# The sums of weights in a Strassen step: four instructions or three, into a tile of their own or in place

## The chip, the cores and the metric

The kernel runs on one core of a Trainium2 chip. The metric is the device time of one execution in microseconds (us), and the median over the runs is compared. A core has five engines with instruction streams of their own: TensorE (PE in the profile; PEld is its loading of the stationary operand), VectorE (DVE), ScalarE (ACT), GpSimd (POOL) and SyncE (SP). Here SP only issues loads from HBM, one after another in one queue.

## The reference, cut to what matters

Two decoder layers over a residual stream h of 256 rows and 2048 columns, all float32. Each layer adds a mixer (attention and mLSTM in layer 0, forgetting attention in layer 1), and then an FFN with 5632 hidden columns. The FFN is where the change lies:

```python
def swiglu(xn, w_gate, w_up, w_down):
    return (jax.nn.silu(xn @ w_gate) * (xn @ w_up)) @ w_down
...
h = h + swiglu(rms_norm(h, norm_ffn[layer]), w_gate[layer], w_up[layer], w_down[layer])
```

So per layer there are three large products: 256 x 2048 by 2048 x 5632 twice, and 256 x 5632 by 5632 x 2048.

## The kernel before, in words

**Products in three parts.** A float32 number is written as a high half, rounded to TensorE's fast fp32r format, and a low half, the rest. A product of two matrices is then three matmuls: high by high, high by low, low by high (`three`, lines 531 to 534; the same in `gemm`, lines 222 to 224). The weights are split as they come in. SP loads a raw tile of 128 partitions and 2 x 512 elements, which is two blocks of 128 rows of the weight side by side (`load_raw`, line 134). ScalarE makes the high half (line 187, or 356 in `split_plain`), VectorE the low half by a subtraction (line 188 or 357). Both halves go into a slot, a pair of tiles named hi and lo. In the FFNs there are eight such slots, and a slot is free again once TensorE has read it.

**Pairs of column blocks.** `pair_group` (lines 539 to 635) makes two blocks of 512 output columns together: one of w_gate and one of w_up, or two of w_down. It goes through the inner dimension in pairs of 128-row blocks; the list `order` says which pair comes at which position, and whether it is a plain one (0) or a Strassen one (1). At a plain position each weight tile is split and multiplied as it is: eight block products of three matmuls. At a Strassen position the 2 x 2 blocks of inputs (two row blocks by two inner blocks) and the 2 x 2 blocks of weights are combined so that seven block products do. The sums of the inputs are made in `sums_of` (lines 272 to 275), once, and used for all columns. The sums of the weights are made anew at each position by VectorE. With a first weight tile `ra` (two inner blocks of the first column block) and a second one `rb`, lines 607 to 610 make ta to td. In the FFNs ta and tb go to a tile of their own, `t4`, and tc and td over `ra`. Then `t4` and `ra` are split like weights. The old `rb` is only read, last by line 609.

At the end `combine` (lines 553 to 570) puts the seven products together from four banks of PSUM: line 555 copies one with ScalarE, and lines 557 to 559 add the others with VectorE.

In the two mixers the same function runs with `halves` given: there the sums are made in place in `ra` and `rb` already, by four instructions, and split into a spare part of the tiles mh and ml. `x95` in the profile is the FFNs' number of Strassen positions, and `x14` and `x6` are the mixers'.

**What sets the order.** The code is written out as a straight line of instructions, and a planner orders each engine's instructions when the program is built, by a priority that follows the text and by a simulated time line; it places the waits too. Waits for a buffer follow from the pools: raw tiles at Strassen positions of the FFN come from the pool's tag "raw" with RAWS buffers (4), raw tiles at plain positions from the pool `wr` with 4 buffers, `t4` has one buffer. The FFN runs in three parts of 3, 4 and 4 column pairs (PARTS, 0, 3, 7, 11; the first of a part is g0): the part's gate and up columns first, then its share of w_down. Of the list ORDER positions 1, 3 and 5 are Strassen ones, and the shorter DOWN[6] of the first part has 1 and 3.

Of the kernel before, what the change touches and what calls it, by code (L numbers as in the profile page):

```python
# [7 lines left out]
F32 = mybir.dt.float32  # L8
# [4 lines left out]
ALU = mybir.AluOpType  # L13
# [4 lines left out]
P = 128  # L18
# [5 lines left out]
NB = 512  # L24
CK = 2
# [11 lines left out]
HEAVY = ((1, 1), (0, 0), (1, 3), (0, 2), (1, 5), (0, 4), (1, 7), (0, 6))  # L37
FOURTH = 7
DENSE = ()
DOWN = {  # L40
    6: ((0, 0), (1, 1), (0, 2), (1, 3), (0, 4), (0, 5)),
    8: ((0, 0), (1, 1), (0, 2), (1, 3), (0, 4), (1, 5), (0, 6), (0, 7)),
# [9 lines left out]
W_RAWS = 4  # L52
LATER = (6, 10, 3, 5)
LATER_DOWN = (5, 6)
RAWS = 4
P_JOIN = 4
COLD = 9
TURNED = (0,)
# [17 lines left out]
def trunk(  # L76
# [19 lines left out]
    nc = tc.nc  # L96
# [141 lines left out]
    sums = {}  # L238
# [24 lines left out]
    def sums_of(pool, sh, sl, copies, full=None, tags=("tmp", "tmp"), bufs=None, box=None, x4=None):  # L263
        if box is not None:
            full, s = box[:, 0:4, :].rearrange("p (i t) q -> p i t q", i=2), box[:, 4:8, :]
            copies(full.rearrange("p i t q -> p i (t q)"))
        elif full is None:
            full = pool.tile([P, 2, NT, P], F32, tag=tags[0], name="full", bufs=bufs)
            copies(full.rearrange("p i t q -> p i (t q)"))
        if box is None:  # L270
            s = pool.tile([P, 4, P], F32, tag=tags[1], name="s4", bufs=bufs)
        nc.vector.tensor_tensor(out=s[:, 0, :], in0=full[:, 0, 1, :], in1=full[:, 1, 1, :], op=ALU.add)
        nc.vector.tensor_tensor(out=s[:, 1, :], in0=s[:, 0, :], in1=full[:, 0, 0, :], op=ALU.subtract)
        nc.vector.tensor_tensor(out=s[:, 2, :], in0=full[:, 0, 0, :], in1=full[:, 0, 1, :], op=ALU.subtract)
# [264 lines left out]
    def pair_group(fp, par, lhs, sums, mats, order, todo=(), halves=None, inner=None, raws=None):  # L539
        plain = [[bank(par, "acc") for _ in range(NT)] for _ in range(2)]  # L540
        begun = set()

# [5 lines left out]
        todo = list(todo)  # L548
# [4 lines left out]
        def combine(prods):  # L553
            c = fp.tile([P, 4, NB], F32, tag="c", name="c", bufs=1)
            nc.scalar.copy(c[:, 0, :], prods[0])
            if halves is None:
                nc.vector.tensor_tensor(out=c[:, 1, :], in0=prods[3], in1=c[:, 0, :], op=ALU.add)
                nc.vector.tensor_tensor(out=c[:, 2, :], in0=prods[2], in1=c[:, 1, :], op=ALU.add)
                nc.vector.tensor_tensor(
                    out=c[:, 1:4:2, :],  # L560
                    in0=prods[1].rearrange("p (a n) -> p a n", a=1).broadcast_to([P, 2, NB]),
                    in1=c[:, 1:3, :],
                    op=ALU.add,
                )
                return c
            nc.vector.tensor_tensor(out=c[:, 2, :], in0=prods[3], in1=c[:, 0, :], op=ALU.add)
            nc.vector.tensor_tensor(out=c[:, 1, :], in0=prods[2], in1=c[:, 2, :], op=ALU.add)
            nc.vector.tensor_tensor(out=c[:, 3, :], in0=prods[1], in1=c[:, 1, :], op=ALU.add)
            nc.vector.tensor_tensor(out=c[:, 2, :], in0=prods[1], in1=c[:, 2, :], op=ALU.add)
            return c  # L570

        for pos, (kind, pair) in enumerate(order):
# [21 lines left out]
            if first:  # L594
                prods = [bank(1 - par, "prod") for _ in range(4)]
            ra, rb = (load_raw(w, k0, c0, NB, fp, W_RAWS if halves else RAWS, raws) for w, c0 in mats)
            hg, lg = split_chunk(ra, NB)
            run_due(todo, pos)
            t4 = ra if halves else fp.tile([P, 2, NB], F32, tag="t4", name="t4", bufs=1)
            ta, tb, tc_, td = (  # L600
                (ra[:, 0, :], rb[:, 0, :], rb[:, 1, :], ra[:, 1, :])
                if halves
                else (t4[:, 0, :], t4[:, 1, :], ra[:, 0, :], ra[:, 1, :])
            )
            hu, lu = slot()
            split_plain(hu[:, 1, :], lu[:, 1, :], rb[:, 1, :])
            nc.vector.tensor_tensor(out=ta, in0=rb[:, 0, :], in1=ra[:, 0, :], op=ALU.subtract)
            nc.vector.tensor_tensor(out=tb, in0=rb[:, 1, :], in1=rb[:, 0, :], op=ALU.subtract)
            nc.vector.tensor_tensor(out=tc_, in0=rb[:, 1, :], in1=ta, op=ALU.subtract)
            nc.vector.tensor_tensor(out=td, in0=ra[:, 1, :], in1=tc_, op=ALU.subtract)  # L610
            parts = []
            for src in (ra, rb) if halves else (t4, ra):
                if halves:
                    hs, ls = halves.pop(0)
                    halves.append((hs, ls))
                else:
                    hs, ls = slot()
                split_plain(hs, ls, src)
                parts.append((hs, ls))
# [17 lines left out]
    def ffn(layer, fp, sx, x4, sd, key, todo, idx_next=None, key_next=None, finish=None):  # L637
# [8 lines left out]
        for g0, g1 in zip(PARTS, PARTS[1:]):  # L646
# [3 lines left out]
            for g in range(g0, g1):  # L650
# [91 lines left out]
            for n0 in (0, 2):  # L742
                if end and idx_next is None and n0 == 2:
                    for n in (2, 3):
                        acc = new_acc()
                        gemm(acc, m_of, wd, n * NB, NB, 0, nk, nk, skew=3 if n == 3 else 1, halved=n == 3)
                        close(acc, n)
                    continue
                plain, c = pair_group(
                    fp, 1 - n0 // 2, m_of, sums_d, [(wd, n0 * NB), (wd, (n0 + 1) * NB)], order, todo  # L750
                )
# [625 lines left out]
```

## Time and profile before

| | us |
|---|---|
| median of three runs | 2077.59 |
| lowest and highest | 2077.39, 2079.51 |
| the profiled execution, its own time | 2077.56 |
| its span, from the first to the last instruction | 2075.9 |
| TensorE busy / VectorE busy / ScalarE busy | 2065.7 / 1819.0 / 1373.7 |
| granted TensorE clock | 0.999 |

How to read the profile: a group's row has the line of the kernel, the engine, the operation, out<-in by the program's names, the shapes and the count; behind the first bar busy time in us and the mean in ns of one; behind the second the engine's idle time just before them and what ended it. A row of the waits view has the waiting instruction, who released it, the total in us, how often, and the longest. A row of the time line has the start and the length in us. A row of the chain has the start, the length and what it was. "lo<-t,hi" is the low half of the tile t4, because buffer numbers are left out of names. Busy times are unions: two instructions that overlap for a moment count once. Layer 0's FFN lies between about 322 and 1010 us of the span, layer 1's begins at about 1380.

### The profile page before, as it was taken

The page shows a single profiled execution, that of the slowest core. Times are in us where ns is not written, and L with a number is a line of the kernel's source. Part 1 is how long each engine was busy: PE and PEld are TensorE (multiplying, and loading weights), DVE is VectorE, ACT ScalarE, POOL GpSimd, SP SyncE. Part 2 cuts the span into 40 slices and gives each one's busy share as a digit, 9 for nine tenths or more (in the row PEclk, how much of TensorE's full clock was granted, in tenths as well). Part 3 has the DMA queues.
Part 4 walks back from the last instruction along what each step waited for, and adds up shares of the span by engine and source line. Part 5 has one row for each costly group of instructions (what it writes and reads, how often), then busy time and mean ns, then how long its engine had stood idle before and what let it go on. Part 6 is the DMA issues. An engine that isn't in the chain of part 4 may idle for free.

```text
span 2075.9 us, 26965 instructions
## 1 busy us (share of the span) xinstructions
PE 2065.7 (100%) x9473; PEld 1715.1 (83%) x9473; DVE 1819.0 (88%) x2367; ACT 1373.7 (66%) x1744; POOL 44.6 (2%) x66
## 2 busy tenths in 40 slices
PE   9999999999999999999999999999999999999998
PEld 7878888888888888888888888888888888888886
DVE  6788769999999999999899688689999999999994
ACT  6777678664676656667676776687655666556763
POOL 1010000000000000000000001000000000000000
PEclk9999999999999999999999999999999999999999
DMA  8566577666677666766676776586756677667764
GB/s 292 169 216 192 188 244 238 206 219 196 210 223 224 193 208 217 222 204 183 206 213 209 231 201 183 155 268 217 233 187 218 209 217 224 202 195 225 206 196 141
DMA packets 309576, 434.88 MB, mean 209 GB/s; under 512 B 106412, under 2 KB 114624, under 8 KB 309312
## 3 DMA queue, kind: packets, MB, share of 16 engines
q1 hardware_dynamic: 307088, 426.27, 66.1%
q0 software_dynamic: 1632, 5.80, 0.8%
q8 instruction: 74, 1.21, 0.2%
q10 hardware_dynamic: 720, 1.09, 0.2%
q14 instruction: 62, 0.51, 0.1%
HBM read 408.68 MB, written 2.12 MB: 198 GB/s over the span
## 4 chain that ended last, share of the span: by engine, by line
PE 97%; DVE 1%; ACT 1%; issue 1%; DMA 0%; POOLq 0%; POOL 0%; ACTq 0%; DVEq 0%
PE acc L532 21%; PE acc L534 21%; PE acc L533 21%; PE acc L223 6%; PE acc L222 6%; PE acc L224 6%; PE prod L532 5%; PE prod L533 5%; PE prod L534 5%; PE p L386 1%; PE po L487 1%; ACT s L420 0%; PE po L488 0%; DVE lo L188 0%; DMA raw<-in_w_down_dram 0%
## 5 line engine op out<-in xcount | busy, mean ns | idle before, releaser
L188 DVE TENSOR_TENSOR lo<-raw,hi 128x1024 fp32r<-128x1024 f32 (+3 forms) x656 | 771.1, 1195 | 135.5 <-ACT hi L187 133.0
L187 ACT CAST hi<-raw 128x1024 fp32r<-128x1024 f32 (+3 forms) x656 | 661.7, 1027 | 341.2 <-PE acc L534 137.2
L533 PE MATMUL acc<-lo,xh 128*128 128x512 f32 x1320 | 514.0, 389 | 0.0
L534 PE MATMUL acc<-hi,xl 128*128 128x512 f32 x1320 | 511.4, 389 | 0.0
L532 PE MATMUL acc<-hi,xh 128*128 128x512 f32 x1320 | 506.2, 390 | 0.0
L534 PEld LDWEIGHTS acc<-hi,xl 128*128 128x128 f32 x1320 | 247.8, 188 | 51.6
L533 PEld LDWEIGHTS acc<-lo,xh 128*128 128x128 f32 x1320 | 247.8, 188 | 51.4 <-issue 0.2
L532 PEld LDWEIGHTS acc<-hi,xh 128*128 128x128 f32 x1320 | 247.7, 188 | 51.3 <-issue 0.2
L356 ACT CAST hi<-raw 128x512 fp32r<-128x512 f32 x204 | 166.9, 819 | 160.7 <-PE acc L534 83.6
L357 DVE TENSOR_TENSOR lo<-raw,hi 128x512 fp32r<-128x512 f32 x204 | 191.6, 939 | 11.4 <-ACT hi L356 10.4
L533 PE MATMUL acc<-lo,mh 128*128 128x512 f32 x466 | 181.0, 389 | 0.0
L534 PE MATMUL acc<-hi,ml 128*128 128x512 f32 x466 | 180.3, 389 | 0.0
L532 PE MATMUL acc<-hi,mh 128*128 128x512 f32 x466 | 176.2, 389 | 0.1
L356 ACT CAST hi<-t 128x1024 fp32r<-128x1024 f32 x95 | 100.0, 1053 | 63.9 <-PE acc L534 38.0
L357 DVE TENSOR_TENSOR lo<-t,hi 128x1024 fp32r<-128x1024 f32 x95 | 116.2, 1224 | 15.2 <-ACT hi L356 15.0
L223 PE MATMUL acc<-lo,mh 128*128 128x512 f32 (+1 forms) x322 | 126.3, 392 | 0.0
L222 PE MATMUL acc<-hi,mh 128*128 128x512 f32 (+1 forms) x322 | 125.8, 391 | 0.0
L224 PE MATMUL acc<-hi,ml 128*128 128x512 f32 (+1 forms) x322 | 123.7, 391 | 0.0
L532 PEld LDWEIGHTS acc<-hi,mh 128*128 128x128 f32 x466 | 87.5, 188 | 18.5 <-ACT hi L187 0.5
L534 PEld LDWEIGHTS acc<-hi,ml 128*128 128x128 f32 x466 | 87.5, 188 | 18.2
L533 PEld LDWEIGHTS acc<-lo,mh 128*128 128x128 f32 x466 | 87.4, 188 | 18.2
L223 PE MATMUL acc<-lo,xh 128*128 128x512 f32 (+3 forms) x288 | 100.0, 348 | 0.2 <-DVE lo L188 0.2
(356 smaller groups left out, 3174.7 us busy)
## 6 DMA issues: line engine op xcount, KB each, us to landing
raw<-in_w_gate_dram SPq DMA_DIRECT2D x176, 512.0 KB, 4.5
raw<-in_w_up_dram SPq DMA_DIRECT2D x176, 512.0 KB, 4.6
raw<-in_w_down_dram SPq DMA_DIRECT2D x176, 512.0 KB, 4.8
raw<-in_w_in_odd_dram SPq DMA_DIRECT2D x88, 512.0 KB, 5.3
raw<-in_w_in_even_dram SPq DMA_DIRECT2D x51, 512.0 KB, 5.1
raw<-in_w_out_even_dram SPq DMA_DIRECT2D x32, 512.0 KB, 5.2
raw<-in_w_out_odd_dram SPq DMA_DIRECT2D x32, 512.0 KB, 4.7
hr<-in_w_in_even_dram SPq DMA_DIRECT2D x12, 512.0 KB, 4.5
```

The costliest lines, as they stand in the source:

```text
L187: latest[0] = nc.scalar.copy(hi[:, k, 0:n], raw[:, k, 0:n])
L188: nc.vector.tensor_tensor(out=lo[:, k, 0:n], in0=raw[:, k, 0:n], in1=hi[:, k, 0:n].bitcast(F32), op=ALU.subtract)
L222: nc.tensor.matmul(o, ah[:, ts], hi, start=(k == 0), stop=False)
L223: nc.tensor.matmul(o, ah[:, ts], lo, start=False, stop=False)
L224: nc.tensor.matmul(o, al[:, ts], hi, start=False, stop=(k == k_all - 1 and cs.stop == n))
L356: nc.scalar.copy(dst_h, src)
L357: nc.vector.tensor_tensor(out=dst_l, in0=src, in1=dst_h.bitcast(F32), op=ALU.subtract)
L386: nc.tensor.matmul(pq[j % 2][:, j // 2, :], q_of(j, b), k_of(j)[:, 0:cols], start=True, stop=True)
L487: nc.tensor.matmul(po, v_of(j, 0), tt[:, j, 0:2, :].rearrange("p c q -> p (c q)"), start=True, stop=False)
L532: nc.tensor.matmul(o, ah, hi, start=start, stop=False)
L533: nc.tensor.matmul(o, ah, lo, start=False, stop=False)
L534: nc.tensor.matmul(o, al, hi, start=False, stop=stop)
```

## The change

At a Strassen position of the FFNs the second column block is taken with a minus sign. With U for the second weight tile and G for the first, the sums are then G0 + U0 (the old ta, negated), that minus U1 (the old tc), and, with one instruction over both halves of `ra`, G0 and G1 minus tc (the old tb, negated, and td). They are made in place: the first two in `rb`, the last two in `ra`. The tile `t4` is no longer used, and the pool of raw tiles has five buffers in place of four. The split takes `rb` first and `ra` second, so that the tile of the first and third sum is the former second weight tile. The signs are made good in `combine` (two additions of prods[1] become subtractions) and in `sums_of` (one difference of inputs is turned round). In the mixers the four instructions stay four with the signs turned. There is also a branch `adding`, in which a load adds the first weight's half to the second's in its place; it is taken from column pair part g0 = 11 on.

```diff
+ADDING = 11
...
-RAWS = 4
+RAWS = 5
...
-        nc.vector.tensor_tensor(out=s[:, 2, :], in0=full[:, 0, 0, :], in1=full[:, 0, 1, :], op=ALU.subtract)
+        nc.vector.tensor_tensor(out=s[:, 2, :], in0=full[:, 0, 1, :], in1=full[:, 0, 0, :], op=ALU.subtract)
...
                     in0=prods[1].rearrange("p (a n) -> p a n", a=1).broadcast_to([P, 2, NB]),
                     in1=c[:, 1:3, :],
-                    op=ALU.add,
+                    op=ALU.subtract,
...
-            nc.vector.tensor_tensor(out=c[:, 3, :], in0=prods[1], in1=c[:, 1, :], op=ALU.add)
-            nc.vector.tensor_tensor(out=c[:, 2, :], in0=prods[1], in1=c[:, 2, :], op=ALU.add)
+            nc.vector.tensor_tensor(out=c[:, 3, :], in0=prods[1], in1=c[:, 1, :], op=ALU.subtract)
+            nc.vector.tensor_tensor(out=c[:, 2, :], in0=prods[1], in1=c[:, 2, :], op=ALU.subtract)
...
+            if adding:
+                (w, c0), part = mats[0], slice(k0 * P, (k0 + 1) * P)
+                nc.gpsimd.dma_start(rb[:, 0, :], w[part, c0 : c0 + NB], accum_op=ALU.add)
             hg, lg = split_chunk(ra, NB)
             run_due(todo, pos)
-            t4 = ra if halves else fp.tile([P, 2, NB], F32, tag="t4", name="t4", bufs=1)
...
             hu, lu = slot()
             split_plain(hu[:, 1, :], lu[:, 1, :], rb[:, 1, :])
-            nc.vector.tensor_tensor(out=ta, in0=rb[:, 0, :], in1=ra[:, 0, :], op=ALU.subtract)
-            nc.vector.tensor_tensor(out=tb, in0=rb[:, 1, :], in1=rb[:, 0, :], op=ALU.subtract)
-            nc.vector.tensor_tensor(out=tc_, in0=rb[:, 1, :], in1=ta, op=ALU.subtract)
-            nc.vector.tensor_tensor(out=td, in0=ra[:, 1, :], in1=tc_, op=ALU.subtract)
-            parts = []
-            for src in (ra, rb) if halves else (t4, ra):
...
+            if halves is None:
+                if not adding:
+                    nc.vector.tensor_tensor(out=rb[:, 0, :], in0=ra[:, 0, :], in1=rb[:, 0, :], op=ALU.add)
+                nc.vector.tensor_tensor(out=rb[:, 1, :], in0=rb[:, 0, :], in1=rb[:, 1, :], op=ALU.subtract)
+                both = rb[:, 1, :].rearrange("p (a n) -> p a n", a=1).broadcast_to([P, CK, NB])
+                nc.vector.tensor_tensor(out=ra, in0=ra, in1=both, op=ALU.subtract)
+                parts = []
+                for src in (rb, ra):
+                    hs, ls = slot()
+                    split_plain(hs, ls, src)
+                    parts.append((hs, ls))
+                where = ((0, 0), (1, 0), (0, 1), (1, 1))
+            else:
+                nc.vector.tensor_tensor(out=ra[:, 0, :], in0=rb[:, 0, :], in1=ra[:, 0, :], op=ALU.add)
+                nc.vector.tensor_tensor(out=rb[:, 0, :], in0=rb[:, 1, :], in1=rb[:, 0, :], op=ALU.subtract)
+                nc.vector.tensor_tensor(out=rb[:, 1, :], in0=ra[:, 0, :], in1=rb[:, 1, :], op=ALU.subtract)
+                nc.vector.tensor_tensor(out=ra[:, 1, :], in0=ra[:, 1, :], in1=rb[:, 1, :], op=ALU.subtract)
...
-            where = ((0, 0), (1, 0), (1, 1), (0, 1)) if halves else ((0, 0), (0, 1), (1, 0), (1, 1))
+                where = ((0, 0), (1, 0), (1, 1), (0, 1))
...
+                    adding=g0 >= ADDING,
```

Here `where` tells from which tile and half each of the four products takes its sum: before, the two products after the three plain ones took both halves of the first tile; now they take the first half of the first tile and the first half of the second.

More of the change, by code (lines that the diff above doesn't have):

```diff
@@ L537, in bank, with pair_group @@
         return pm.tile([P, NB], F32, tag="pm", name=name) if par else pa.tile([P, NB], F32, tag="acc", name=name)
-    def pair_group(fp, par, lhs, sums, mats, order, todo=(), halves=None, inner=None, raws=None):
+    def pair_group(fp, par, lhs, sums, mats, order, todo=(), halves=None, inner=None, raws=None, adding=False):
         plain = [[bank(par, "acc") for _ in range(NT)] for _ in range(2)]
@@ L596, in pair_group @@
             ra, rb = (load_raw(w, k0, c0, NB, fp, W_RAWS if halves else RAWS, raws) for w, c0 in mats)
+            if adding:
+                (w, c0), part = mats[0], slice(k0 * P, (k0 + 1) * P)
+                nc.gpsimd.dma_start(rb[:, 0, :], w[part, c0 : c0 + NB], accum_op=ALU.add)
             hg, lg = split_chunk(ra, NB)
             run_due(todo, pos)
-            t4 = ra if halves else fp.tile([P, 2, NB], F32, tag="t4", name="t4", bufs=1)
[L600 to L604, printed above, removed]
@@ L605, in pair_group @@
             hu, lu = slot()
             split_plain(hu[:, 1, :], lu[:, 1, :], rb[:, 1, :])
[L607 to L610, printed above, removed]
-            parts = []
-            for src in (ra, rb) if halves else (t4, ra):
-                if halves:
+            if halves is None:
[15 more added lines that the diff above has]
+                nc.vector.tensor_tensor(out=ra[:, 1, :], in0=ra[:, 1, :], in1=rb[:, 1, :], op=ALU.subtract)
+                parts = []
+                for src in (ra, rb):
@@ L614, in pair_group @@
                     hs, ls = halves.pop(0)
                     halves.append((hs, ls))
[L616 to L619, printed above, removed]
-            where = ((0, 0), (1, 0), (1, 1), (0, 1)) if halves else ((0, 0), (0, 1), (1, 0), (1, 1))
+                    split_plain(hs, ls, src)
+                    parts.append((hs, ls))
+                where = ((0, 0), (1, 0), (1, 1), (0, 1))
             ht = [parts[a][0][:, b, :] for a, b in where]
@@ L749, in ffn @@
                 plain, c = pair_group(
-                    fp, 1 - n0 // 2, m_of, sums_d, [(wd, n0 * NB), (wd, (n0 + 1) * NB)], order, todo
+                    fp, 1 - n0 // 2, m_of, sums_d, [(wd, n0 * NB), (wd, (n0 + 1) * NB)], order, todo, adding=g0 >= ADDING
                 )
```

## The prediction, made before the result was known

> **What bounds the kernel now.** I read the page's first two parts, then the busy time by stage, then who waits for whom, then the chain in the only place where the matmuls pause, and last the groups of the instructions that change.
>
> ```profile
> span 2075.9 us, 26965 instructions
> PE 2065.7 (100%) x9473; PEld 1715.1 (83%) x9473; DVE 1819.0 (88%) x2367; ACT 1373.7 (66%) x1744; POOL 44.6 (2%) x66
> DVE  6788769999999999999899688689999999999994
> ```
>
> TensorE is busy for the whole span, but VectorE (DVE) is at 9 tenths in nearly every slice of the two FFNs, so the page alone does not say which of the two sets the pace. The stages do:
>
> ```profile
> 420.00:460.00 40.00, 40.00 (x179) 33.10 (x178) 39.25 (x50) 27.55 (x31) 0.00 (x0) 1.00 0.74 234
> 760.00:860.00 100.00, 100.00 (x443) 82.80 (x442) 94.06 (x113) 61.56 (x68) 0.00 (x0) 1.00 0.65 206
> 1720.00:1820.00 100.00, 100.00 (x443) 82.81 (x442) 92.35 (x106) 57.80 (x63) 0.00 (x0) 1.00 0.64 202
> 469.53 0.39 PE L533 MATMUL acc<-lo,mh 128*128 128x512 f32 x1
> 469.75 0.39 PE L534 MATMUL acc<-hi,ml 128*128 128x512 f32 x1
> 470.26 0.50 PE L532 MATMUL acc<-hi,mh 128*128 128x512 f32 x1
> 470.59 0.40 PE L533 MATMUL acc<-lo,mh 128*128 128x512 f32 x1
> ```
>
> The columns of the first three rows are the stretch, its length, then the busy time of PE, PEld, DVE, ACT and POOL with their counts. Two stretches of 100 us, one in each layer, hold the same 443 matmuls: 100 / 443 = 0.226 us from one to the next, and the last four rows show what that looks like: a matmul every 0.22 to 0.23 us (the 0.39 us is the length of one in the pipeline), and a single pause of 0.51 - 0.227 = 0.28 us. That pause at 470 us (0.39 us with the slower step behind it, 0.33 instead of 0.227) is the only one that I found in either FFN. In the same stretches DVE has 100 - 94.1 = 5.9 and 7.7 us idle. So TensorE's own issue sets the time, and DVE is second, close behind. Who waits confirms it:
>
> ```profile
> PE cold L170 <- POOL ones L167: 1.2, 1, 1.2
> PE acc L223 <- DVE lo L188: 0.2, 1, 0.2
> PE acc L222 <- ACT hi L785: 0.2, 1, 0.2
> ACT hi L187 <- PE acc L534: 137.4, 94, 4.6
> ACT hi L356 <- PE acc L534: 121.9, 93, 3.0
> ```
>
> The first three rows are everything that the waits view has for PE: nothing in the FFNs. The last two say that ScalarE, which makes the high half of every weight chunk, waits 137.4 + 121.9 = 259 us for TensorE to give back a weight slot. The makers are ahead, held by full buffers.
>
> How far ahead, in one weight pair in the middle and in the tightest one:
>
> ```profile
> 601.84 1.22 DVE L357 TENSOR_TENSOR lo<-t,hi 128x1024 fp32r<-128x1024 f32 x1 [0.24 <-ACT hi L356]
> 607.05 1.22 DVE L357 TENSOR_TENSOR lo<-raw,hi 128x1024 fp32r<-128x1024 f32 x1
> 611.60 0.39 PE L533 MATMUL prod<-lo,sx 128*128 128x512 f32 x1
> 613.19 0.39 PE L533 MATMUL prod<-lo,sx 128*128 128x512 f32 x1
> ...
> 462.88 1.22 DVE L357 TENSOR_TENSOR lo<-t,hi 128x1024 fp32r<-128x1024 f32 x1 [0.33 <-ACT hi L356]
> 466.36 0.39 PE L533 MATMUL prod<-lo,sd 128*128 128x512 f32 x1
> ```
>
> The low half of the first sum tile is done at 603.06 and read at 611.60, 8.5 us later; that of the second is done at 608.27 and read at 613.19, 4.9 us later. In the first down group the first is done at 464.10 and read at 466.36: 2.3 us.
>
> **The change part by part.** It acts at each Strassen position of the FFNs, 95 in all.
>
> ```profile
> L610 DVE TENSOR_TENSOR raw<-raw 128x512 f32<-128x512 f32 x109 | 75.5, 693 | 0.6
> L609 DVE TENSOR_TENSOR raw<-raw,t 128x512 f32<-128x512 f32 x95 | 65.7, 691 | 0.5
> L607 DVE TENSOR_TENSOR t<-raw 128x512 f32<-128x512 f32 x95 | 65.6, 690 | 11.7 <-DMA raw<-in_w_down_dram 3.3 <-DMA raw<-in_w_up_dram 2.8 <-DVE lo L357 1.9
> L608 DVE TENSOR_TENSOR t<-raw 128x512 f32<-128x512 f32 x95 | 65.5, 690 | 0.0
> L559 DVE TENSOR_TENSOR c<-prod,c 128x1024 f32<-128x1024 f32 x33 | 40.4, 1223 | 0.0
> 464.94 0.68 DVE L607 TENSOR_TENSOR t<-raw 128x512 f32<-128x512 f32 x1
> 465.54 0.69 DVE L608 TENSOR_TENSOR t<-raw 128x512 f32<-128x512 f32 x1
> 466.14 1.22 DVE L188 TENSOR_TENSOR lo<-raw,hi 128x1024 fp32r<-128x1024 f32 x1
> 467.28 0.69 DVE L357 TENSOR_TENSOR ml<-pf,mh 128x512 fp32r<-128x512 f32 x1
> 859.68 0.69 DVE L609 TENSOR_TENSOR raw<-raw,t 128x512 f32<-128x512 f32 x1
> 860.40 0.69 DVE L610 TENSOR_TENSOR raw<-raw 128x512 f32<-128x512 f32 x1
> ```
>
> *Four instructions become three.* Removed are L607 to L610, 0.690 + 0.690 + 0.691 + 0.693 = 2.76 us by duration. Added are two of 128x512 and one of 128x1024 with one operand repeated. L559 is such an instruction already (one operand repeated over 1024): 1.223. So 2.61 us, 0.16 less, 95 x 0.16 = 15 us of DVE's busy time. But neighbours overlap: starts at 464.94, 465.54, 466.14, 467.28 are 0.60 us apart behind a 512 and 1.14 behind a 1024, so the engine's own time falls from 4 x 0.60 = 2.40 to 2 x 0.60 + 1.14 = 2.34, by 0.06 us, 95 x 0.06 = 6 us in all.
>
> *A chain in place.* The old L607 and L608 read only loaded data and did not depend on each other. The new three hang together: the second reads what the first wrote and must let the low split of the same half pass, the third reads what the second wrote. Where L610 follows L609, whose result it reads, the starts are 860.40 - 859.68 = 0.72 us apart, not 0.60: 0.12 us for a dependent neighbour. Up to three such steps are at hand, so an upper end of 2.34 + 0.36 - 2.40 = +0.30 us per position; the lower end is -0.06. The planner puts other work between most such pairs (at 465.54 the next one is a plain split), and the old code paid at some pairs too; I take about one step, +0.06, near nothing, 95 x 0.06 = +6 us of an engine with 5.9 us idle in every 100. All of it is hidden behind TensorE as long as that idle time lasts; ends for DVE over the whole kernel: -6 and +29 us.
>
> The Trainium skill's page VectorE: DVE Perf Modes, section The DRAIN you can't avoid, says that a semaphore between chained Vector instructions costs nothing extra, and its rules for kernel authors say to minimize the count of operations, not of semaphores. By that page the step would be free and the change would save DVE 6 us. The two starts at 859.68 and 860.40 against those at 464.94 and 465.54 disagree: 0.72 against 0.60 us.
>
> *Later and sooner.* The first tile to be split is now the former second weight block, with both sums that hang on the chain; before, the first tile needed only loaded data. Its low half is ready later, by at most the lead of the first over the second tile in the old order, 608.27 - 603.06 = 5.2 us in the middle. There it had 8.5, so 3.3 stay. The second tile is now read by the fifth product of the seven and not by the sixth: three matmuls, 0.68 us sooner, out of 4.9. In the first down group 2.3 us are there, and the two subtractions that now stand ahead of the split are 0.60 + 1.14 = 1.7: 0.6 stay, if the order is otherwise the same. Cost nothing, bounds 0 and +1 us in each layer.
>
> *Buffers and queues.* t4 goes, a fifth raw tile takes its place (both 128x1024 f32). The block that L609 released now lives until its split, but a load waits for the tile five loads back, not four. SP's queue is held mainly by the other pool, the plain tiles (the last row here counts the positions in the stretch from 330 to 460 us):
>
> ```profile
> SPq L134 <- DVE lo L188: 774.5, 408, 13.5
> SPq L134 <- DVE raw L609: 153.5, 63, 5.5
> ...
> L609 DVE TENSOR_TENSOR raw<-raw,t 128x512 f32<-128x512 f32 x10 | 6.9, 692 | 0.0
> ```
>
> 774.5 us against 153.5. A raw load that goes earlier meets the next plain load in the same queue, so little changes. The stall at 470 us is of that kind:
>
> ```profile
> 460.23 1.06 ACT hi L187
> 461.32 1.24 DVE lo L188
> 462.57 5.61 DMA raw<-in_w_down_dram
> 468.20 0.04 ACT hi L187
> ```
>
> A plain split on DVE freed a tile at 462.55, its load took 5.61 us, and TensorE was short by 0.39 us. DVE had 40 - 39.25 = 0.75 us idle in the 40 us before, so what DVE gains or loses per position there  arrives here: over 10 positions 10 x -0.06 removes the stall, +0.06 adds up to 0.6. Bounds -0.39 and +3.0.
>
> *The rest costs nothing.* The subtractions in the combination (L559, L568, L569) and the operands exchanged in L274 are the same instructions with another sign. In the mixers' branch four instructions stay four, with the same dependences. The branch with an adding load is never taken: it wants g0 of at least 11, and g0 is 0, 3 or 7. ScalarE's casts stay four per position.
>
> **Sum.** TensorE's matmuls are the same. From the profiled execution's 2077.56 us (span 2075.9, 1.66 outside it), about half of the 0.39 us goes: **2077.4 us**. The median of the runs shown is 2077.59, the profiled one 0.03 below it.
>
> **The rivals.**
>
> 1. *DVE becomes the bound at the head of each FFN (slower).* Place: from 330 to 470 us and the same groups of layer 1, where DVE has 0.75 us idle in 40. If all three dependent steps are paid, each position costs 0.30 more; 10 of them are 3.0 us in a layer, 6.0 in both: 2083.6 us. It decides from about 0.2 us per position, when the idle time there (3 or 4 positions in those 40 us) is used up. For it speaks the saturated row 420 to 460; against it, that the steps are filled by other work and that there are weights in stock.
> 2. *TensorE isn't really full, and DVE's 6 to 15 us come off (faster).* PEld is busy 83% only, so 17% could be open: 2077.56 - 6 to - 15 = 2062.6 to 2071.6 us. The Trainium skill (Trainium Kernel Development and Optimization, section Performance Expectations) says just that: matmul busy time is a bad metric, and weight-load busy time a good one. But in both stretches without a pause PEld is at 82.8 too; that is its full mark here, since one matmul of 512 columns lasts longer than a load. The trace speaks against it.
> 3. *The planner lays out another order.* The order of every engine comes from a schedule made when the program is built, and three instructions with other lengths shift it. The stall at 470 us exists in layer 0 and not in layer 1 with the same code, so the order makes or removes stalls of such a size. A few of them: 2076.6 to 2080 us.
> 4. *The change doesn't do what it says.* Were the adding load taken, the count of instructions would show it; with g0 of 0, 3 and 7 it can't be. No chance of its own.
>
> **How the numbers follow.** Forecast case (2076.9 to 2078.5): 0.75. Rival 1, from 2079 to 2083.6: 0.12, half of it over the line. Rival 2: 0.03. Rival 3: 0.10, most of it within the line. The line is 0.2%, 4.2 us, about what a measurement of this kernel can tell from no change (2073.4 and 2081.7). Faster 0.03 (rival 2), slower 0.08 (half of rival 1 and a little of 3), the same 0.89. The range takes in the forecast, rival 3 and the lower half of rival 1: 2076.4 to 2081.0.
>
> **What would show it.** Right: DVE's busy time falls by about 15 us, the matmuls in a 100 us stretch stay 443, PE has no new row in the waits view, the pause near 470 us is shorter or gone. The three new instructions: two of 0.69 and one of 1.22 us, 95 times each. Wrong: PE rows that wait for DVE's low halves in 330 to 500 or 1380 to 1560 us (rival 1), a duration far from 1.22 for the repeated operand, matmul counts above 443 (rival 2), or pauses in the mixers, where nothing was edited but signs (rival 3).

## The result, and the profile after

The changed kernel is slower: a median of 2094.35 us (2092.05 to 2094.91, four runs) against 2077.49 us for the kernel before, run on the same chip (2077.12 to 2079.51, four runs). The ratio is 1.0077 with a 95% interval of 1.006 to 1.0095: 16.9 us. The profiled execution took 2092.05 us, 14.5 us more than the profiled one of before.

Lines have moved by one: the casts L187 and L356 are now L188 and L357, the low halves L188 and L357 are L189 and L358, the three matmuls L532 to L534 are L533 to L535. The sums are now L607 (G0 + U0), L608 (that minus U1, over U1) and L610 (both halves of G minus that, 1024 elements wide). First the page of the changed kernel, its span, busy times and the shares of its chain:

```profile
span 2090.3 us, 26784 instructions
PE 2071.6 (99%) x9473; PEld 1715.4 (82%) x9473; DVE 1817.5 (87%) x2272; ACT 1362.4 (65%) x1744; POOL 46.1 (2%) x66
PE 71%; DVE 14%; DMA 7%; issue 4%; ACT 4%; SPq 0%; ACTq 0%; DVEq 0%; POOLq 0%; POOL 0%
```

The matmuls are the same 9473, the span is 14.4 us longer, and VectorE is busy 1.5 us less. So the work has not grown. The chain that ended last tells more: before, it was 97% TensorE and 1% VectorE (page of before), now 14% of it runs over VectorE and 7% over transfers. Taking, from one matmul's start to the next, what exceeds the usual (median) step of its shape by more than 0.05 us, and adding that up over the span, gives 23.8 us of pauses before and 37.9 after: 14.1 us, nearly the whole difference of the spans. In the two FFNs alone there is under 1 us before and 15.5 after, so the loss is made there. Where the pauses lie, from the busy times by stretch (columns as in the prediction), first before, then after:

```profile
330.00:380.00 50.00, 50.00 (x223) 41.39 (x222) 48.51 (x69) 39.35 (x51) 0.13 (x1) 1.00 0.69 212
650.00:760.00 110.00, 110.00 (x487) 91.10 (x486) 101.91 (x119) 67.24 (x73) 0.00 (x0) 1.00 0.68 215
860.00:960.00 100.00, 100.00 (x443) 82.78 (x442) 92.84 (x113) 70.24 (x77) 0.00 (x0) 1.00 0.73 225
1380.00:1430.00 50.00, 50.00 (x222) 41.39 (x222) 45.62 (x67) 41.71 (x58) 0.70 (x1) 1.00 0.70 209
```

```profile
330.00:380.00 50.00, 47.77 (x211) 39.20 (x210) 46.14 (x63) 37.58 (x51) 0.33 (x1) 1.00 0.65 200
650.00:760.00 110.00, 107.48 (x471) 87.73 (x470) 97.68 (x108) 66.74 (x73) 0.00 (x0) 1.00 0.66 207
860.00:960.00 100.00, 100.00 (x443) 82.87 (x442) 94.23 (x108) 70.31 (x77) 0.00 (x0) 1.00 0.67 208
1380.00:1430.00 50.00, 48.40 (x212) 39.39 (x211) 43.37 (x62) 38.95 (x55) 0.70 (x1) 1.00 0.76 217
```

Between 860 and 960 us nothing has changed: 443 matmuls in 100 us, as before. Between 650 and 760 us there are 471 where there were 487, and VectorE's busy time falls there too, from 101.91 to 97.68. An engine that had become the bound by its load would be busier in the stretch that lost time. This one stands still more. The waits view of TensorE has rows for it now:

```profile
PE acc L533 <- ACT hi L188: 3.5, 3, 2.2
PE prod L534 <- DVE lo L358: 2.0, 3, 1.7
PE prod L533 <- DVE h L371: 1.4, 2, 0.8
```

The first row is taken up further below. The longest of the second row is the pause at 709 us. This is the time line of VectorE around it, and then that of TensorE:

```profile
706.62 1.22 DVE L358 TENSOR_TENSOR lo<-raw,hi 128x1024 fp32r<-128x1024 f32 x1
709.52 0.69 DVE L607 TENSOR_TENSOR raw<-raw 128x512 f32<-128x512 f32 x1 [1.68 <-DMA raw<-in_w_down_dram]
710.13 1.22 DVE L358 TENSOR_TENSOR lo<-raw,hi 128x1024 fp32r<-128x1024 f32 x1
```

```profile
709.31 0.39 PE L535 MATMUL prod<-hi,sd 128*128 128x512 f32 x1
711.40 0.50 PE L534 MATMUL prod<-lo,sd 128*128 128x512 f32 x1 [1.70 <-DVE lo L358]
```

TensorE waits 1.70 us for the low half that VectorE begins at 710.13. Its cast had ended at 707.34, and VectorE was done with the split before it at 707.84. But ahead of it in VectorE's order stands L607 at 709.52: the first sum of the *next* position, and it waits 1.68 us for the load of its own second weight tile. VectorE kept to its order here, so work that was due at once waited behind work that TensorE needed only some 20 us later, because the latter waited for a transfer. The groups of the three new instructions show that this is not one case:

```profile
L610 DVE TENSOR_TENSOR raw<-raw 128x1024 f32<-128x1024 f32 x95 | 115.8, 1219 | 1.3
L607 DVE TENSOR_TENSOR raw<-raw 128x512 f32<-128x512 f32 x95 | 65.2, 686 | 50.8 <-DMA raw<-in_w_up_dram 23.9 <-DMA raw<-in_w_down_dram 13.6 <-issue 12.9
L608 DVE TENSOR_TENSOR raw<-raw 128x512 f32<-128x512 f32 x95 | 65.1, 686 | 1.3
```

VectorE stands idle ahead of the first sum for 50.8 us in all, at 43 of the 95 positions; before it was 11.7. Following the 95 positions through the trace, each with its load, its sums, its splits and the matmul that reads them first, gives these means, good to about 0.2 us:

| us | before | after |
|---|---|---|
| second tile landed to first sum | 6.5 | 0.8 |
| second tile landed to TensorE's first read of the first sum tile | 27.5 | 27.4 |
| low half of the first sum tile done to its first read | 8.7 | 4.05 |
| low half of the second sum tile done to its first read | 6.8 | 3.6 |
| the lowest tenth of these two leads, up to about | 4.7 / 3.7 | 1.0 / 0.6 |

The loads of the second tiles are not late: they land 27 us ahead of use, as before. But the first sum has moved to the very landing of its load, 5.7 us earlier, while the splits have moved 4.6 and 3.2 us nearer to TensorE. Who ScalarE waits for has changed as well, rows of before first:

```profile
ACT hi L356 <- DVE raw L610: 67.2, 32, 5.0
ACT hi L187 <- DMA raw<-in_w_down_dram: 30.8, 25, 3.8
ACT hi L187 <- PE prod L534: 19.0, 16, 2.6
ACT hi L187 <- DMA raw<-in_w_up_dram: 16.4, 16, 1.9
ACT hi L356 <- PE prod L534: 13.1, 8, 4.5
```

```profile
ACT hi L357 <- DVE raw L608: 132.5, 43, 6.6
ACT hi L188 <- PE acc L535: 82.9, 44, 5.8
ACT hi L188 <- PE prod L535: 49.5, 19, 4.6
ACT hi L188 <- DMA raw<-in_w_down_dram: 45.1, 28, 6.3
ACT hi L357 <- PE acc L535: 42.1, 26, 3.9
ACT hi L188 <- DMA raw<-in_w_up_dram: 35.8, 22, 4.2
ACT hi L357 <- DVE raw L610: 17.6, 25, 1.4
```

It waits for slots 82.9 + 49.5 + 42.1 = 174.5 us, where it was 19.0 + 13.1 and the 259.3 of the prediction, 291.4 us. For VectorE's sums it waited before too, 67.2 us for the last one; now it is 132.5 + 17.6 us, most of it for the second. The stock of split weights, which hid everything before, is mostly gone.

The waits for loads have grown as well, from 30.8 + 16.4 to 45.1 + 35.8 us: these are loads of plain tiles and of first weight tiles, which the table does not follow. One of a plain tile ends the longest pause of all, 2.4 us at 353 us, the first row of TensorE's waits. From the chain in that window:

```profile
349.17 1.22 DVE lo L189
350.39 0.03 DVE s L273
350.42 4.55 DMA raw<-in_w_gate_dram
...
355.05 1.05 ACT hi L188
356.10 0.04 issue
356.14 0.50 PE acc L533
```

The load went out as a split on VectorE ended, and this split stood in VectorE's order behind all three sums of a position (L607 at 345.83, L608 and L610). VectorE itself did not stand still there. The pause at 1420 us (1.3 us) has the same chain. So the pauses have two faces: a split that is late because VectorE waits ahead of it, and a plain tile whose load goes out late because the split ahead of it is late in VectorE's order. How the 15.5 us divide between the two was not measured.

### The profile page after: what moved, and what is told of

It reads as the page before. It is cut to its first block, busy times and chain, and to the rows that moved or that the text cites. A ratio compares the mean times of both kernels' runs of the same rounds, so it can differ in the third digit from the quotient of the medians.

```text
span 2090.3 us, 26784 instructions
## 1 busy us (share of the span) xinstructions
PE 2071.6 (99%) x9473; PEld 1715.4 (82%) x9473; DVE 1817.5 (87%) x2272; ACT 1362.4 (65%) x1744; POOL 46.1 (2%) x66
## 4 chain that ended last, share of the span: by engine, by line
PE 71%; DVE 14%; DMA 7%; issue 4%; ACT 4%; SPq 0%; ACTq 0%; DVEq 0%; POOLq 0%; POOL 0%
PE acc L534 15%; PE acc L535 15%; PE acc L533 15%; DVE lo L189 5%; PE acc L223 4%; PE acc L224 4%; PE acc L225 4%; PE prod L534 3%; PE prod L533 3%; PE prod L535 3%; DVE lo L358 3%; DMA raw<-in_w_up_dram 3%; DMA raw<-in_w_down_dram 3%; ACT hi L188 2%; DVE raw L610 1%
## 5 line engine op out<-in xcount | busy, mean ns | idle before, releaser
L189 DVE TENSOR_TENSOR lo<-raw,hi 128x1024 fp32r<-128x1024 f32 (+3 forms) x656 | 771.7, 1191 | 121.6 <-ACT hi L188 119.1
L188 ACT CAST hi<-raw 128x1024 fp32r<-128x1024 f32 (+3 forms) x656 | 659.4, 1025 | 325.7 <-PE acc L535 82.7
L534 PE MATMUL acc<-lo,xh 128*128 128x512 f32 x1320 | 514.8, 390 | 0.5 <-DVE lo L189 0.5
L535 PE MATMUL acc<-hi,xl 128*128 128x512 f32 x1320 | 512.6, 390 | 0.0
L533 PE MATMUL acc<-hi,xh 128*128 128x512 f32 x1320 | 507.0, 391 | 3.4 <-ACT hi L188 3.4
L357 ACT CAST hi<-raw 128x1024 fp32r<-128x1024 f32 (+1 forms) x299 | 264.7, 891 | 209.7 <-DVE raw L608 132.5
L358 DVE TENSOR_TENSOR lo<-raw,hi 128x1024 fp32r<-128x1024 f32 (+1 forms) x299 | 304.1, 1023 | 12.5 <-ACT hi L357 12.4
L533 PEld LDWEIGHTS acc<-hi,xh 128*128 128x128 f32 x1320 | 247.9, 188 | 55.5 <-ACT hi L188 4.2
L534 PEld LDWEIGHTS acc<-lo,xh 128*128 128x128 f32 x1320 | 248.0, 188 | 52.3 <-DVE lo L189 0.9
L535 PEld LDWEIGHTS acc<-hi,xl 128*128 128x128 f32 x1320 | 248.0, 188 | 51.2
L534 PE MATMUL acc<-lo,mh 128*128 128x512 f32 x466 | 182.1, 391 | 0.5 <-DVE lo L358 0.5
L535 PE MATMUL acc<-hi,ml 128*128 128x512 f32 x466 | 180.7, 390 | 0.0
L533 PE MATMUL acc<-hi,mh 128*128 128x512 f32 x466 | 175.8, 391 | 0.3 <-ACT hi L188 0.2
L610 DVE TENSOR_TENSOR raw<-raw 128x1024 f32<-128x1024 f32 x95 | 115.8, 1219 | 1.3
L607 DVE TENSOR_TENSOR raw<-raw 128x512 f32<-128x512 f32 x95 | 65.2, 686 | 50.8 <-DMA raw<-in_w_up_dram 23.9
L534 PEld LDWEIGHTS acc<-lo,mh 128*128 128x128 f32 x466 | 87.5, 188 | 20.1 <-DVE lo L358 1.4
L533 PEld LDWEIGHTS acc<-hi,mh 128*128 128x128 f32 x466 | 87.5, 188 | 19.3 <-ACT hi L188 1.2
L535 PEld LDWEIGHTS acc<-hi,ml 128*128 128x128 f32 x466 | 87.5, 188 | 18.0
```

Source lines behind the costliest of these rows:

```text
L188: latest[0] = nc.scalar.copy(hi[:, k, 0:n], raw[:, k, 0:n])
L189: nc.vector.tensor_tensor(out=lo[:, k, 0:n], in0=raw[:, k, 0:n], in1=hi[:, k, 0:n].bitcast(F32), op=ALU.subtract)
L357: nc.scalar.copy(dst_h, src)
L358: nc.vector.tensor_tensor(out=dst_l, in0=src, in1=dst_h.bitcast(F32), op=ALU.subtract)
L533: nc.tensor.matmul(o, ah, hi, start=start, stop=False)
L534: nc.tensor.matmul(o, ah, lo, start=False, stop=False)
```

## The experiments

Four theories were weighed; the expectations call them by their letters.

- **A, the place of the first sum.** Before, the first sums went into `t4`, whose one buffer could not be written before the last position's tile was split. In place, only the load holds the sum back; it is ordered at its load's landing and blocks the splits behind it.
- **B, the three instructions.** The chain of dependent sums and the long last one load VectorE more than four separate ones (the prediction's rival 1).
- **C, buffers.** Without `t4` the raw tiles of the Strassen positions are held longer, and their loads come later.
- **D, overwriting.** The second sum is written over U1, so it must let U1's cast and low split pass first, and these may wait for a slot.

The first four runs share their runs of the kernel before (2077.55 us), the next four theirs (2077.39), the last two theirs (2077.81). Diffs are against the changed kernel unless told otherwise.

**The three instructions, with t4 kept.** Only signs and the merged third instruction remain of the change.

```diff
-RAWS = 5
+RAWS = 4
...
-                if not adding:
-                    ...(out=rb[:, 0, :], in0=ra[:, 0, :], in1=rb[:, 0, :], op=ALU.add)
-                ...(out=rb[:, 1, :], in0=rb[:, 0, :], in1=rb[:, 1, :], op=ALU.subtract)
...
+                t4 = fp.tile([P, 2, NB], F32, tag="t4", name="t4", bufs=1)
+                ...(out=t4[:, 0, :], in0=ra[:, 0, :], in1=rb[:, 0, :], op=ALU.add)
+                ...(out=t4[:, 1, :], in0=t4[:, 0, :], in1=rb[:, 1, :], op=ALU.subtract)
...
-                for src in (rb, ra):
+                for src in (t4, ra):
```

> The changed kernel with its three instructions and signs, but the first two sums go to the tile t4 of their own again (one buffer) and the raw pool has four buffers. Theory A (order): in the changed kernel nothing but its load holds back the first sum, so the planner puts it so early in VectorE's fixed order that it waits there for its load and holds up the splits behind it; with t4 it is held back again: 2077 to 2080 us, idle time before the first sum back to 10 to 15 us. Theory B (chain): the three dependent instructions ahead of both splits eat the lead; they are all still there: 2088 to 2095 us. Theory C (buffers): the second raw tile is held longer and loads come late; here it is free again early: 2077 to 2080 us.

Measured: 2078.38 us, ratio 1.0005 (0.9996 to 1.0015): the whole loss is gone. Its groups and its waits of ScalarE:

```profile
L610 DVE TENSOR_TENSOR raw<-raw,t 128x1024 f32<-128x1024 f32 x95 | 115.6, 1217 | 0.7
L607 DVE TENSOR_TENSOR t<-raw 128x512 f32<-128x512 f32 x95 | 65.0, 684 | 0.7 <-DMA raw<-in_w_down_dram 0.3
```

```profile
ACT hi L188 <- PE acc L535: 137.0, 109, 4.0
ACT hi L357 <- PE acc L535: 131.6, 101, 2.3
ACT hi L357 <- DVE raw L610: 44.2, 21, 4.3
```

The idle time before the first sum is 0.7 us, ScalarE waits for slots again, and the leads of the two splits are 8.7 and 7.7 us. The dependent chain and the merged instruction, as long as in the changed kernel, cost nothing in this order. B falls as the cause of the loss, which hangs on the tile of its own. Nor does this version gain on the kernel before: TensorE sets the time of both.

**In place, but four instructions.** The merged instruction is undone, the rest stays.

```diff
-                both = rb[:, 1, :].rearrange("p (a n) -> p a n", a=1).broadcast_to([P, CK, NB])
-                nc.vector.tensor_tensor(out=ra, in0=ra, in1=both, op=ALU.subtract)
+                for a in range(CK):
+                    nc.vector.tensor_tensor(out=ra[:, a, :], in0=ra[:, a, :], in1=rb[:, 1, :], op=ALU.subtract)
```

> The changed kernel in place, but with the last two sums as two instructions of 128x512 in place of one of 128x1024. Theory A: as slow as the changed kernel, 2089 to 2097 us, since the first sum stands where it stood. Theory B: if the merged instruction is the cost, faster by most of the loss, 2077 to 2084; if it is the chain as such, as slow. Theory C: as slow, 2089 to 2097 us.

Measured: 2088.45 us, ratio 1.0057 (1.0042 to 1.0072). The group of the first sum:

```profile
L607 DVE TENSOR_TENSOR raw<-raw 128x512 f32<-128x512 f32 x95 | 65.3, 687 | 47.5 <-DMA raw<-in_w_up_dram 19.2 <-DMA raw<-in_w_down_dram 14.6 <-issue 9.1
```

Most of the loss stays with the idle time, so what is done in place is what costs. It is 5.9 us faster than the changed kernel, though, and no theory had that number.

**The first sum behind the low split of U1, or behind the last position's split.** Two ways to take the first sum away from its load's landing, with no other edit (the planner orders everything anew around it). What stands under `tc.issue_after(x)` is put behind x in the order; `low_u` is what `split_plain` now returns, its subtraction. The second is the hold that `t4`'s one buffer gave.

```diff
-            split_plain(hu[:, 1, :], lu[:, 1, :], rb[:, 1, :])
+            low_u = split_plain(hu[:, 1, :], lu[:, 1, :], rb[:, 1, :])
...
-                if not adding:
+                with tc.issue_after(low_u.ins):
```

> The changed kernel with one edge more: the first sum stands behind the low split of the same second weight tile in VectorE's order. Same instructions, buffers and signs. Theory A: the loss goes, 2076 to 2080 us, idle time before the first sum under 5 us. Theory B: the chain starts later and nothing of it is shorter: as slow or slower, 2091 to 2100 us. Theory C: loads and buffers as in the changed kernel: 2089 to 2097 us.

```diff
-                if not adding:
+                with tc.issue_after(held[0].ins) if held else ExitStack():
...
-                    split_plain(hs, ls, src)
+                    lows.append(split_plain(hs, ls, src))
...
+                held[:] = lows[:1]
```

> The changed kernel with another edge: the first sum stands behind the split of the first sum tile of the Strassen position before, which is what the one buffer of t4 used to force. Theory A: most of the loss goes, 2077 to 2083 us. Theories B and C: 2089 to 2097 us.

Measured: 2083.97 us, ratio 1.0033 (1.0021 to 1.0044), and 2084.10 us, ratio 1.0034 (1.0021 to 1.0047). In both the idle time before the first sum is 0.0 us and 10.3 to 10.4 of the 16.9 us are gone. That is A, but less than A wanted (2076 to 2080 and 2077 to 2083 us): 6.5 us stay. In the first of the two ScalarE still waits for the second sum:

```profile
L607 DVE TENSOR_TENSOR raw<-raw 128x512 f32<-128x512 f32 x95 | 64.8, 682 | 0.0
```

```profile
ACT hi L357 <- DVE raw L608: 95.9, 34, 4.6
```

The leads are 5.0 and 4.7 us, not the 8.7 and 7.7 of the version with `t4`. That was the reason for theory D.

**t4 kept, and the second sum made to wait as overwriting makes it.** The first experiment's kernel with one order added:

```diff
-                nc.vector.tensor_tensor(out=t4[:, 1, :], in0=t4[:, 0, :], in1=rb[:, 1, :], op=ALU.subtract)
+                with tc.issue_after(low_u.ins):
+                    nc.vector.tensor_tensor(out=t4[:, 1, :], in0=t4[:, 0, :], in1=rb[:, 1, :], op=ALU.subtract)
```

> The kernel of e1 (three instructions, t4 kept, four raw buffers) with one edge: the second sum stands behind the low split of the second weight tile in VectorE's order, which is what writing it in place forces (it overwrites the half that this split and its cast read). Theory D: in place, the second sum, and with it ScalarE's cast of the first sum tile, has to wait until the cast and the low split of that half have run, and these wait for a slot from TensorE; so the sums can no longer be made ahead: the wait of ScalarE for that sum goes from 5 us to about 100 us, 2081 to 2086 us. Theory A alone (only the first sum's place matters; e3 and e4 kept a rest of 6.5 us for another reason): 2077 to 2080 us.

Measured: 2081.80 us, ratio 1.0021 (1.0011 to 1.003), 3.4 us above the first experiment. In its waits of ScalarE the second sum (L609 here) is back; in the first experiment it had 5.2 us:

```profile
ACT hi L357 <- DVE t L609: 105.5, 47, 4.1
```

So the order alone, with no overwriting and with all buffers of before, makes this wait and 3.4 us of loss. That bears D out; that the same order costs as much in place is an inference.

**The sums of before, with t4 from the pool of raw tiles.** The kernel before with two edits, so that the single buffer's hold goes, and nothing else:

```diff
-RAWS = 4
+RAWS = 5
...
-            t4 = ra if halves else fp.tile([P, 2, NB], F32, tag="t4", name="t4", bufs=1)
+            t4 = ra if halves else fp.tile([P, 2, NB], F32, tag="raw", name="t4", bufs=RAWS)
```

> The kernel before with its four instructions, in which the tile t4 is taken from the pool of raw tiles (five buffers in all, three in use at a position) and no longer has one buffer of its own. Not in place, no merged instruction. Theory A: the first sum is no longer held back by one buffer and may stand at its load's landing: idle time before it 25 us or more, 2080 to 2090 us. Theory D: nothing is overwritten, 2076 to 2080 us, unless loads come late for want of buffers.

Measured: 2080.00 us, ratio 1.0013 (1.0004 to 1.0023). The idle time that A wanted did not come:

```profile
L607 DVE TENSOR_TENSOR t<-raw 128x512 f32<-128x512 f32 x95 | 65.6, 691 | 13.2 <-DMA raw<-in_w_down_dram 6.9 <-DMA raw<-in_w_up_dram 6.0
```

The first sum stayed 5.1 us behind its load's landing (6.5 before). A miss: a looser hold is not yet none, since this `t4` still waits for a tile of the pool, while the sum in place waits for the load alone. Its 2.6 us over the kernel before are not explained either. ScalarE waits 115.1 us behind the last sum here, though nothing is overwritten, so a wait of this size behind a sum is no proof of D by itself:

```profile
ACT hi L356 <- DVE raw L610: 115.1, 39, 5.4
```

That the one buffer *by itself* kept the order is therefore not shown. Shown is that a hold of this kind, put back into the version in place, takes the 10 us away.

**The low split of U1 written ahead.** The pinned version, with U1's cast and split in the text ahead of the first weight tile's:

```diff
+            if halves is None:
+                hu, lu = slot()
+                low_u = split_plain(hu[:, 1, :], lu[:, 1, :], rb[:, 1, :])
             hg, lg = split_chunk(ra, NB)
             run_due(todo, pos)
-            hu, lu = slot()
-            low_u = split_plain(hu[:, 1, :], lu[:, 1, :], rb[:, 1, :])
+            if halves:
+                hu, lu = slot()
+                split_plain(hu[:, 1, :], lu[:, 1, :], rb[:, 1, :])
```

> The kernel of e3 (in place, first sum behind the low split) with the cast and low split of the second weight's half written ahead of those of the first weight tile, so that they take a slot sooner and the in-place overwrite can follow sooner. Theory D: the second sum comes earlier, ScalarE's wait for it falls from 96 to under 60 us, 2078 to 2082 us. If the rest of 6.5 us is the chain of three dependent instructions as such, no change: 2082 to 2086 us.

Measured: 2080.70 us, ratio 1.0018 (1.0008 to 1.0027): 3.3 us less than without it, the time that D gave. But the wait by which it should have come did not shrink (the second sum is L612 here):

```profile
ACT hi L357 <- DVE raw L612: 99.6, 38, 6.0
```

The time is D's, the mechanism's own number is not (95.9 before, under 60 expected), so this run does not show that D is why; the leads rose to 5.9 and 4.9 us.

**Pinned, with four instructions.** Both edits together: the first sum behind the low split, the merged instruction undone.

> The kernel of e3 with the last two sums as two instructions of 128x512. If the merged instruction costs time by itself, as the 5.9 us between e2 and the changed kernel suggest: 2077 to 2080 us. If that difference came from the planner's order alone: 2082 to 2087 us.

Measured: 2084.08 us, ratio 1.0035 (1.0021 to 1.0048), against 2083.97 with the merged one. The merged instruction costs and saves nothing here. The 5.9 us that it seemed to cost unpinned are then most likely the order that the planner makes around it; which step of that order was not found.

**Four raw tiles.** The change without its fifth tile (`RAWS = 4`).

> The changed kernel with four raw buffers and not five. Theory C (buffers set the loss): with one fewer the second tile's load goes later still and the loss grows, 2098 to 2110 us, and it lands less far ahead of its use than the 27 us of the changed kernel. Theories A and D (order and overwriting): the first sum stands at its load's landing already and no load is short of time, so little changes: 2090 to 2098 us.

Measured: 2095.96 us, ratio 1.0087 (1.007 to 1.0103), 1.6 us above the change. The group of the first sum:

```profile
L607 DVE TENSOR_TENSOR raw<-raw 128x512 f32<-128x512 f32 x95 | 65.5, 689 | 67.1 <-DMA raw<-in_w_up_dram 52.4 <-DMA raw<-in_w_down_dram 12.6 <-DVE sd L358 1.7
```

Here the second tiles do land later (23.4 us ahead of use, not 27.4), VectorE stands 16 us longer, and still it costs only 1.6 us. So neither the number of raw tiles nor VectorE's idle time as such sets the loss. C falls as the cause.

**The load adds.** `ADDING = 0` in place of 11: the first sum is made by the load, and VectorE has no L607 at all.

> The changed kernel with its branch for an adding load taken everywhere: the first sum is made by a load that adds the first weight's half to the second's, issued from GpSimd's queue, and VectorE makes two sums only. Theory A: VectorE no longer stands before the first sum, so that part of the loss (about 10 us) goes; the second sum waits for the adding load instead, behind the low split: 2080 to 2086 us. If the adding load, which starts only once the second tile has landed, comes too late for the second sum, the loss stays: 2090 to 2105 us.

Measured: 2081.77 us, ratio 1.0017 (1.0008 to 1.0027). Its page and its waits of ScalarE:

```profile
PE 2066.3 (99%) x9473; PEld 1714.4 (82%) x9473; DVE 1769.7 (85%) x2177; ACT 1366.7 (66%) x1744; POOL 125.6 (6%) x161
```

```profile
ACT hi L357 <- DVE raw L608: 95.2, 36, 6.1
```

With the blocking instruction gone, 12.6 of the 16.9 us go. That VectorE has 47.8 us less to do buys nothing beyond that: the time stays 4.0 us above the kernel before, and ScalarE's wait for the second sum stays, as D wants, though here that sum also waits for the adding load.

## Why the prediction was wrong

Shown is that the whole loss of 16.9 us comes with making the sums in place: with `t4` kept it is gone. Its parts are less sure. About 10 us: the first sum stands in VectorE's order at its load's landing, ahead of splits that are due (the two pinned versions; the version with the adding load agrees). Of the other 6.5 us about 3.4 fit the second sum's wait for the overwritten half's split (the second sum pinned with `t4` kept, +3.4; the split written ahead, -3.3, without the shorter wait that was to explain it). About 3 us of the rest stay open, and with them the 5.9 us by which four instructions are faster in the unpinned order.

Point by point:

- **What bounds the kernel: right.** TensorE sets the time, and 443 matmuls in 100 us is its pace: where nothing pauses, the changed kernel has the same count. Three instructions with `t4` kept come out at 2078.38 us, the forecast's own case (2076.9 to 2078.5).
- **Four instructions become three: durations right.** 0.686, 0.686 and 1.219 us were forecast as 0.69, 0.69 and 1.22 (2.60 in all, where the step added up 2.61). That VectorE's busy time would fall by 15 us was wrong, and by the step's own words: busy times are unions, so what counts is the engine's time, for which -6 to +29 us was given. It fell by 1.5 us, and by 1.4 in the version with `t4` kept.
- **A chain in place: size right, mechanism incomplete.** In the time line of the changed kernel the second sum and the merged one, which reads its result, start 0.72 us apart:

```profile
702.05 0.69 DVE L608 TENSOR_TENSOR raw<-raw 128x512 f32<-128x512 f32 x1
702.77 1.23 DVE L610 TENSOR_TENSOR raw<-raw 128x1024 f32<-128x1024 f32 x1
```

  The Trainium skill's page VectorE: DVE Perf Modes, section The DRAIN you can't avoid, says that a semaphore between chained Vector instructions costs nothing extra. For these sums this trace doesn't agree either: 0.72 us to a dependent neighbour against 0.60 to an independent one. It decides nothing here. The step also wrote that the second sum "must let the low split of the same half pass", and priced only the 0.12 us of a neighbour. What the second sum with `t4` kept shows to cost, 3.4 us, is not the neighbour but its being late: by theory D the split waits for a cast, the cast for a slot, and ScalarE's next cast waits for the sum.
- **"Later and sooner": the step that failed.** It reckoned 3.3 us of lead left in the middle and 0.6 in the first down group, "if the order is otherwise the same", and took the cost as nothing, at most 1 us in each layer. The order was not the same: the first sum came 5.7 us sooner after its load, and the lead of the first tile is 4.05 us on the mean, with about a tenth of the positions at some 1 us or less; the two FFNs lost 14.6 us in pauses. Nor did TensorE read the second tile three matmuls sooner: at 709 us it is the third of the three sum products, not the second, that waits for it.
- **"Buffers and queues": wrong by what it left out.** It weighed `t4` as space, and its loss as a question of when loads come. In that it was right: the second tiles land as early as before, and a tile less costs 1.6 us. But the tile was also a hold on the order of VectorE, and the step did not ask what holds the first sum once it is gone. Its reading of SP's queue left out the row `SPq L134 <- DVE lo L357: 244.1, 102, 7.0`, in which raw tiles are given back too; nothing in the outcome hangs on it.
- **Rival 1** had the sign and two of the places (330 to 380 us and 1380 to 1430), and neither the mechanism nor the bound: the pauses are also at 709 and at 1775 us, VectorE is less busy at 650 to 760 us than before, and the same three dependent instructions cost nothing with `t4` kept. Its sign came, but small: TensorE waits for low halves 0.2 us in 330 to 500 us and 0.8 us in 1380 to 1560; for ScalarE's casts (L188) it waits 2.2 and 1.3 us there. **Rival 2** falls with the version with `t4` kept; weight loads are at 82.87 us in a full stretch of 100, as in the prediction, so the 17% that the Trainium skill's rule on them (Trainium Kernel Development and Optimization, section Performance Expectations) would leave open isn't open here either. **Rival 3** named the right actor, the planner's order, and took its price from the one stall of before, 0.39 us; the runs show 10 us and more. **Rival 4**: the adding load was not taken, as said; the instructions fell from 2367 to 2272, by 95.

The range ended at 2081.0 because the only price it held for a new order was a stall that the old order had.

## What to carry to other kernels

A tile of its own can also be a hold on an engine's order: here, once it was gone, the planner put the sum at the landing of its load, and what was due behind it stood until the transfer was done. Before an instruction is moved in place, ask what holds it from then on, where in the engine's order that puts it, and who stands behind it there; its duration says nothing on that. A sum written over its operand also waits for the slowest reader of the old content, so write that reader ahead, or keep the tile.

## What the runs showed of the hardware

One thing was not expected. SP issues not only loads from HBM: its queue is also held by transposes between tiles. The time line of SP shortly before the pause at 709 us:

```profile
694.82 5.34 SPq L708 DMA_TRANSPOSE turned<-c  x4
700.26 3.15 SPq L135 DMA_DIRECT2D raw<-in_w_down_dram  x4
```

Four transposes occupy the queue for 5.34 us, some 1.3 us each; a plain issue just before them, at 690.03, took 0.37 us. The load for which L607 waits at 709.52 went out behind them, as the last but one of the four plain issues, at 702.48. The last transpose was done at 700.17, though, and in the view of SP's waits the two loads ahead of it wait for VectorE's splits (L189 and L358). So how much of that pause is due to the transposes isn't shown.
